# Hybrid decoder layer: the beginning and the cross attention in a written order, the memory's norm behind its projection, and the mLSTM's first gate chain and products at later places

## The chip, the cores and the metric

The kernel runs on one core of a Trainium2 chip. The metric is device time in microseconds (us) from one launch to its end, as a median over runs. The core has a matrix engine (TensorE, PE in the profile, whose weight loads are listed as PEld), a vector engine (VectorE, DVE), an engine for activations (ScalarE, ACT), a general one (GpSimd, POOL), and SyncE (SP), which here issues nearly all transfers. Every engine works through its own queue of instructions in order and waits on semaphores.

## The reference

One decoder layer on a sequence of 1024 tokens of width 1024 and a memory of 256 tokens, all in float32:

```python
h = rms_norm(x, norm_mix_g)
mq, mk, mv, mi, mf, mo, dq, dk, dv, cq = split(h @ w_in)
y_m = sigmoid(mo) * rms_norm(mlstm_chunkwise(silu(conv(mq, mk)), mv, mi, mf))   # 4 heads, chunks of 128
y_d = diff_attention(dq, dk, dv)                                                 # 8 heads, causal
mkv = rms_norm(mem, mem_norm_g) @ w_mem_kv
y_c = cross_attention(rms_norm(cq), rms_norm(mkv[:, :512]), mkv[:, 512:])        # 4 heads of 128, values 256 wide
g_m, g_d, g_c = split(sigmoid(h @ w_gate + b_gate))
x = x + (g_m * (y_m @ w_proj_m) + g_d * (y_d @ w_proj_d) + g_c * (y_c @ w_proj_c)) @ w_out
x = x + square(relu(rms_norm(x) @ w_up)) @ w_down
```

`rms_norm(v, g)` is v · rsqrt(mean(v²) + 1e-6) · g over the last axis. The change touches the norms of x and of the memory, the projection of the memory, cross attention, and the order in the mLSTM.

## The kernel before

**Split products.** A product of two float32 matrices is done in three passes (`mm3`, L121): each operand is split into a high part, rounded to fp32r, and a low part, the rest; PE adds high·high, high·low and low·high in PSUM. `split` (L111) and `split2` (L102) make the parts: ACT writes the high part (L115, or L118 with a scale), then DVE subtracts (L116, or L119). `load_w` (L142) loads a weight group in four raw pieces by SP (ring `rp`, 3 buffers) and splits each into a buffer of `wp` (4 buffers). Below, a "product" is one pass, one PE instruction of 512 columns in most places.

**Stages.** `consts` (L194) loads the vectors and transposes them, and computes lambda. `phase_x` (L299) is the beginning: it loads both tiles of memory (`mx`), normalises their rows in place (`norm_rows`, L240: a square on ACT with a sum, a power on POOL in `rsqrt_mean`, a multiply on DVE), and calls `mem_kv` (L248). That transposes the memory into `memT`, splits it with the norm's gain as scale, and projects it in three groups of 512 columns: one of K (`kr`, squared, normalised per head, transposed into `mkT`) and two of V (`mv`). x is loaded in eight tiles (`xk`), normalised row by row, and `half` transposes four tiles at a time into `hT`, the split and transposed h, in eight steps of 128 features. A score tile `sc` in PSUM holds two of these steps. Between the halves stands the second group of V's weights.

`branch_c` (L342) is cross attention. A stream of PE work (the query projection of eight tiles of 128 tokens, then 32 steps of merge-gate products) is cut into positions: a position is the three passes of one k. At positions given by a table, `weave` (L493) puts `turn` (normalised queries transposed), `scores` (L378: products, row maximum, four exponentials into `cpe`, and the softmax's division on DVE), `ptr` (the probabilities of one head transposed into `cpT`) and `values` (their product with `mv`, one score tile for each 128 columns, stored to HBM).

`branch_m` (L583) is the mLSTM, again a stream with a table. Its stream projects v, q and k and the output gates; the first 264-wide weight holds the input and forget gates too. `m_gates` (L505) begins with two transposes of `gi` and `gf` on PE and runs a long chain on DVE, ACT and two round trips through HBM, whose results are `g_b`, `g_w` and `g_a`, and rows that are stored to HBM (`g_dng`, `g_dwi`, `g_dd`) and loaded again. `m_gates2` (L575) transposes the three into `g_col`. Each of the eight half heads n then has items at a base position e plus an offset: `inter` (queries times the inter-chunk weight, `qp`), `decays` (the mask rows `ngb`), `krows` (weighted keys, `ks`), `scores`, four `chunk`s and three `final`s. `sc<-va,ks` and `sc<-va,mpT` are a chunk's state update and its numerator.

Behind these come the rest of the gates, the differential attention, the merge and the MLP, which the change leaves alone.

**What sets the order.** Instructions go through a scheduler that may reorder them within an engine unless they are kept in program order. In the kernel before, PE alone is pinned, and that in `branch_c` and `branch_m`; the order of ACT, DVE, SP and POOL, and PE's in the beginning, is the scheduler's. Buffers are handed out in rings (`rings`, L129), and a tile can be written once the readers of the one that had its buffer are done.

Of the kernel before, what the change touches and what calls it, by code (L numbers as in the profile page):

```python
# [71 lines left out]
class Layer:  # L72
    def __init__(self, tc, a, out):
        self.tc, self.nc, self.a, self.out = tc, tc.nc, a, out
        self.V, self.A = tc.nc.vector, tc.nc.scalar
        self.n = 0
# [117 lines left out]
    def consts(self, tmp):  # L194
# [32 lines left out]
        lv = tmp.tile([P, 256], F32, name="lamv")  # L227
        nc.sync.dma_start(lv, a["lamv"].partition_broadcast(P))
        pr = tmp.tile([P, 128], F32, name="lamp")
        l4 = lv.rearrange("p (a b) -> p a b", a=4)  # L230
        nc.vector.tensor_mul(pr[:, 0:64], l4[:, 0], l4[:, 1])
# [7 lines left out]

    def norm_rows(self, src, r1, scr):  # L240

        nc = self.nc
        nc.scalar.activation(scr, src, AF.Square, accum_out=r1)
        self.rsqrt_mean(r1, r1, D, 1)
        nc.vector.tensor_scalar_mul(src, src, r1)


    def mem_kv(self, pool, tmp, xs):  # L248
        nc, a = self.nc, self.a
        memT = tmp.tile([P, NK, 2, 256], F32R, tag="memT", name="memT")  # L250
        for k in range(0, NK, 2):
            ps = self.tp_tile()
            for i in range(2):
                for t in range(2):
                    nc.tensor.transpose(
                        ps[:, (i * 2 + t) * P : (i * 2 + t + 1) * P], xs[t][:, (k + i) * P : (k + i + 1) * P], self.ident
                    )
            for i in range(2):
                self.split(
                    memT[:, k + i, 0], memT[:, k + i, 1], ps[:, i * 256 : (i + 1) * 256],  # L260
                    self.vec[:, R_MEM + k + i : R_MEM + k + i + 1],
                )
        self.mkT = pool.tile([P, 4, 2, 256], F32R, name="mkT")
        self.mv = pool.tile([P, 2, 2, D], F32R, name="mv")

        def proj(w, t):
            ps = self.mm_tile()
            for k in range(NK):
                self.mm3(
                    ps, (memT[:, k, 0, t * P : (t + 1) * P], memT[:, k, 1, t * P : (t + 1) * P]), w[k], k == 0, k == NK - 1  # L270
                )
            return ps
# [26 lines left out]
    def phase_x(self, kv, tmp):  # L299
# [14 lines left out]
        for x in mem:  # L314
            norm(x)
# [1508 lines left out]
```

## Time and profile before

| | us |
|---|---|
| median of 3 runs | 2248.64 |
| lowest and highest | 2246.41, 2258.45 |
| the profiled execution | 2249.61 |
| its span, first to last instruction | 2247.8 |
| mean granted clock of TensorE | 0.993 |

All times in what follows are of the profiled execution unless a run is named. A row of the timeline gives start, length, engine, line, operation, output and inputs, shapes and count; what stands in brackets at its end is the engine's idle time ahead of it and who ended that. In a window's row, PEclk is the clock that TensorE was granted, in parts of full speed. The stages of the kernel before lie in the trace like this: the beginning to about 66 us, cross attention to 183, the mLSTM behind it.

### The profile page before, as it was taken

The numbers are of one execution on the slowest core, as the hardware profiler recorded it, in microseconds if no ns is written. First come the engines' busy times: TensorE is split into PE (matmuls) and PEld (weight loads), VectorE is DVE, ScalarE is ACT, GpSimd is POOL, SyncE is SP. The second block draws the span as 40 slices with busy tenths as digits, with TensorE's granted clock in tenths as the row PEclk, the third lists the DMA queues.
The fourth block names the chain that finished last, engine by engine and source line by source line (L and its number), as shares of the span: only waits on it lengthen the run. The fifth ranks groups of instructions, "written<-read, shape, count | busy, mean of one in ns | idle before, by whom it ended". The sixth has DMA issues, their size and how long they took to land.

```text
span 2247.8 us, 30530 instructions
## 1 busy us (share of the span) xinstructions
PE 2182.6 (97%) x11222; PEld 1877.5 (84%) x11222; DVE 1398.3 (62%) x2627; ACT 1019.8 (45%) x1994; POOL 540.4 (24%) x696
## 2 busy tenths in 40 slices
PE   7999899999999999999999999999899999899999
PEld 5778788988899999999888888887788888688777
DVE  6645366655138888888752232544588777865688
ACT  6533355444236666666542120323445444543232
POOL 2100000000011111111100002202666665665553
PEclk9999999999999999999999999999999999999999
DMA  6013122111311111110133443436445444844434
GB/s 246 20 71 113 44 87 78 54 60 52 119 55 34 34 31 38 38 36 29 61 128 135 134 148 117 141 103 206 153 143 186 151 155 162 296 163 147 154 118 169
DMA packets 113781, 247.89 MB, mean 110 GB/s; under 512 B 11066, under 2 KB 19551, under 8 KB 111583
## 3 DMA queue, kind: packets, MB, share of 16 engines
q1 hardware_dynamic: 111326, 233.36, 31.5%
q10 hardware_dynamic: 2304, 12.58, 1.4%
q8 instruction: 88, 1.44, 0.3%
q14 instruction: 63, 0.51, 0.1%
HBM read 178.76 MB, written 67.14 MB: 109 GB/s over the span
## 4 chain that ended last, share of the span: by engine, by line
PE 68%; DVE 14%; DMA 8%; ACT 5%; issue 2%; POOL 2%; SPq 0%; DVEq 0%; ACTq 0%; POOLq 0%
PE mm L91 40%; PE p L91 18%; PE sc L91 4%; PE tp L94 2%; PE po L91 2%; DVE sc L67 1%; DMA wraw<-in_wdown 1%; ACT dpe L67 1%; DVE wo L105 1%; DVE dpe L67 1%; PE pr L94 1%; DVE draw L67 1%; DVE dst L67 1%; DMA xr<-h_d 1%; DVE w L116 1%
## 5 line engine op out<-in xcount | busy, mean ns | idle before, releaser
L91 PE MATMUL mm<-hT,w 128*128 128x512 f32 x1920 | 466.4, 397 | 0.5 <-ACT gt L488 0.5
L91 PE MATMUL mm<-w,hT 128*128 128x384 f32 (+3 forms) x2496 | 459.3, 330 | 1.9 <-ACT w L115 1.6
L91 PEld LDWEIGHTS mm<-hT,w 128*128 128x128 f32 x1920 | 356.1, 189 | 76.0 <-ACT gt L488 1.7
L91 PEld LDWEIGHTS mm<-w,hT 128*128 128x128 f32 x2496 | 389.6, 189 | 12.1 <-ACT w L115 2.3
L91 PE MATMUL p<-xd,wo 128*128 128x512 f32 x1344 | 313.3, 394 | 16.5 <-DVE acc L1619 9.4
L91 PEld LDWEIGHTS p<-xd,wo 128*128 128x128 f32 x1344 | 253.5, 190 | 76.2 <-DVE acc L1619 12.8
L91 PE MATMUL p<-xo,wo 128*128 128x512 f32 x1344 | 309.5, 392 | 6.2 <-DVE st L1473 4.2
L91 PEld LDWEIGHTS p<-xo,wo 128*128 128x128 f32 x1344 | 253.2, 189 | 61.2 <-ACT pt L1286 4.6
L91 PE MATMUL mm<-kt,w 128*128 128x512 f32 x1152 | 261.8, 389 | 0.5 <-DVE w L116 0.5
L91 PEld LDWEIGHTS mm<-kt,w 128*128 128x128 f32 x1152 | 216.1, 188 | 46.1 <-DVE w L116 1.0
L104 ACT CAST wo<-wraw 128x896 fp32r<-128x896 f32 x122 | 114.9, 942 | 190.3 <-PE p L91 126.8
L105 DVE TENSOR_TENSOR wo<-wraw,wo 128x896 fp32r<-128x896 f32 x122 | 146.2, 1212 | 49.9 <-ACT wo L104 49.8
L1200 POOL TENSOR_TENSOR wraw<-wraw 128x128 f32<-128x128 f32 x128 | 99.0, 773 | 212.3 <-DMA wraw<-in_wdown 132.2
L115 ACT CAST w<-raw 128x256 fp32r<-128x256 f32 (+2 forms) x144 | 86.4, 619 | 140.1 <-PE mm L91 103.7
L67 ACT ACTIVATE dpe<-sc,dst,drr 128x256 f32<-128x256 f32 (+7 forms) x128 | 106.7, 833 | 62.2 <-DVE dst L67 51.6
L116 DVE TENSOR_TENSOR w<-raw,w 128x256 fp32r<-128x256 f32 (+2 forms) x144 | 100.5, 718 | 52.3 <-ACT w L115 52.3
L105 DVE TENSOR_TENSOR xd<-xd 128x1536 fp32r<-128x1536 f32 (+2 forms) x36 | 69.0, 1922 | 70.5 <-ACT xd L104 70.5
L67 DVE CUSTOM_DVE_ANT_0 sc<-sc,tmask 128x256 f32<-128x256 f32 (+7 forms) x128 | 97.0, 758 | 3.6 <-PE sc L91 2.4
L139 POOL TENSOR_SCALAR hss<-hss 128x4 f32<-128x4 f32 x8 | 3.3, 415 | 398.5 <-ACT mscr L767 398.5
L1201 POOL TENSOR_TENSOR wraw<-wraw 128x128 f32<-128x128 f32 x128 | 96.9, 757 | 0.0
L1202 POOL TENSOR_TENSOR wraw<-wraw 128x128 f32<-128x128 f32 x128 | 94.2, 736 | 0.0
L104 ACT CAST xd<-xd 128x1536 fp32r<-128x1536 f32 (+2 forms) x36 | 54.9, 1528 | 73.0 <-DMA xd<-r_d 73.0
(324 smaller groups left out, 3161.1 us busy)
## 6 DMA issues: line engine op xcount, KB each, us to landing
wraw<-in_wup SPq DMA_DIRECT2D x64, 256.0 KB, 3.2
r_d<-xts SPq DMA_DIRECT2D x16, 1024.0 KB, 4.3
wraw<-in_wdown SPq DMA_DIRECT2D x64, 256.0 KB, 3.1
xd<-r_d SPq DMA_DIRECT2D x19, 768.0 KB, 7.6
xd<-r_d SPq DMA_DIRECT2D x14, 1024.0 KB, 6.3
raw<-in_wgate SPq DMA_DIRECT2D x48, 256.0 KB, 3.0
gates<-gt SPq DMA_DIRECT2D x48, 256.0 KB, 2.1
raw<-in_wd SPq DMA_DIRECT2D x32, 384.0 KB, 3.1
```

The costliest lines, as they stand in the source:

```text
L67: return self.tc.keep_in_program_order(f(*a, **k))
L91: self.pin(self.nc.tensor.matmul(out, l, r, start=start, stop=stop))
L94: self.pin(self.nc.tensor.transpose(out, x, self.ident))
L104: self.A.copy(hi, src)
L105: low = lambda: self.V.tensor_sub(lo, src, f32(hi))
L115: nc.scalar.copy(hi, src)
L116: nc.vector.tensor_sub(lo, src, f32(hi))
L139: g.tensor_scalar(r, ss, 1.0 / width, EPS, op0=ALU.mult, op1=ALU.add)
L1200: G.tensor_add(r[:, 4], r[:, 0], r[:, 3])
L1201: G.tensor_sub(r[:, 5], r[:, 4], r[:, 1])
L1202: G.tensor_sub(r[:, 6], r[:, 1], r[:, 0])
```

## The change

It has four parts. The numbers of instructions stay as they were, but for a few on DVE.

**A written order.** A wrapper `InOrder` for SP, DVE and ACT keeps each instruction in program order. `phase_x` and `branch_c` use it, and `split2`, `split2s` and the new `w_raw` and `w_split` issue through it. The whole beginning is written out by hand:

```diff
+        w, rm = [], []
+        mem_turn(0)
+        w += self.w_split(raws[0][0], 512, 2)
+        mem_turn(2)
+        ps = [self.mm_tile() for _ in range(2)]
+        for k in range(NK):
+            for t in range(2):
+                proj(ps[t], w, k, t)
+            if k % 2 == 0 and k < 6:
+                w += self.w_split(raws[0][k // 2 + 1], 512, 2)
+                if k < 4:
+                    mem_turn(k + 4)
+            if k in (3, 5):
+                rm.append(square(mem[k // 4], "rm"))
...
+        rx = [square(x) for x in xs[0:4]]
+        for x, r in zip(xs, rx):
+            V.tensor_scalar_mul(x, x, r)
...
+        w = self.w_split(raws[1][0], 512, 2)
+        turn2(0, 0)
+        turn2(0, 2)
...
+            if k in (3, 5):
+                turn2(0, k + 1)
+                kr_turn(k // 4)
+            if k >= 4:
+                rx.append(square(xs[k]))
+            if k >= 6:
+                V.tensor_scalar_mul(xs[k - 2], xs[k - 2], rx[k - 2])
+        w2 = self.w_split(raws[2][0], 512, 2)
+        for i in (6, 7):
+            V.tensor_scalar_mul(xs[i], xs[i], rx[i])
```

`mem_turn(k)` transposes and splits two steps of memory, `turn2(hf, k)` two steps of x into one score tile, and `kr_turn` one tile of K. Cross attention's query weights are loaded and split here too, `wp` has 5 buffers, and lambda's arithmetic stands behind the beginning.

**The memory's norm behind its projection.** The raw memory is transposed, and the row's scale `rm` comes in where the products leave PSUM: as the scale of the copy and square of K, and of both parts of `mv` (`split2s`). K's four multiplies per tile become one with a broadcast.

**Cross attention.** `scores` ends with the exponentials; `probs`, the division, is an item of its own. Both value products of a head share one 1024-wide score tile. `cpe` has 8 buffers in place of 6, the first gate weights are loaded by eight items, and the first weights of the mLSTM may be loaded while cross attention runs (`self.wp.i = 11`).

```diff
+            add(8 * t + 21, probs, t)
+        for k in range(NK):
+            add(41 + 2 * k + k // 2, self.gate_load)
         for hf in range(2):
             for h in range(4):
-                b = (43, 78)[hf] + (4, 5)[hf] * h
+                b = (48 + 8 * h, 80 + 4 * h)[hf]
                 add(b, ptr, hf, h, 0)
-                add(b + 1, ptr, hf, h, 1)
-                add(b + 5, values, hf, h, 0)
-                add(b + 5, values, hf, h, 1)
+                add(b + 2 - hf, ptr, hf, h, 1)
+                add(b + 5 - 2 * hf, values, hf, h)
```

**The mLSTM's table.** Seven positions more for `m_gates2`, and other offsets for the first half head, with `decays` ahead of `inter`; three DVE instructions are pinned there, and the ones columns of `va` are written later.

```diff
-        add(96 + 8, self.m_gates2, gp)
+        add(96 + 15, self.m_gates2, gp)
...
-            kt, st, ch, fi = (9, 2, 14, 34) if n == 0 else (-2, 2, 7, 33) if n == 1 else (-16, -8, 3, 29)
+            kt, st, ch, fi = (18, 22, 26, 42) if n == 0 else (-2, 2, 7, 33) if n == 1 else (-16, -8, 3, 29)
...
-                add(e + 9, inter, hd, hf)
-                add(e + 9, decays, hd, hf)
-                st = 10
+                add(e + 16, decays, hd, hf)
+                add(e + 16, inter, hd, hf)
```

Where instructions stand now is shown at three places. First DVE's queue around the norm of x's second half, before: `xk` rows are the scaling of a tile of x, `hT` and `mv` rows low parts, `w_638` a weight's low part.

```order
L245 TENSOR_SCALAR xk_329<-xk_329,r_70_491 128x1024
L119 SCALAR_TENSOR_TENSOR hT<-sc_385,vec,hT 128x512
L119 SCALAR_TENSOR_TENSOR hT<-sc_398,vec,hT 128x512
L245 TENSOR_SCALAR xk_331<-xk_331,r_72_497 128x1024
L245 TENSOR_SCALAR xk_333<-xk_333,r_74_503 128x1024
L116 TENSOR_TENSOR mv<-mm_561,mv 128x512
L116 TENSOR_TENSOR w_638<-raw_636,w_638 128x1024
```

And the same place after, where `xk_270` and `xk_272` are the seventh and eighth tile and `w_482` is the first weight of V's second half.

```order
L67 TENSOR_TENSOR mkT<-tp_446,mkT 128x4x128
L67 TENSOR_SCALAR xk_266<-xk_266,r_66_422 128x1024
L67 TENSOR_SCALAR xk_268<-xk_268,r_70_453 128x1024
L67 TENSOR_TENSOR w_482<-raw_274,w_482 128x1024
L67 TENSOR_SCALAR xk_270<-xk_270,r_72_464 128x1024
L67 TENSOR_SCALAR xk_272<-xk_272,r_74_476 128x1024
L67 SCALAR_TENSOR_TENSOR mv<-mm_359,rm_221,mv 128x512
```

The weight's low part moved from behind all scalings to a place ahead of the last two.

Second ACT's queue at x's first half, before, with `hT` rows the high parts and the number behind `sc` the buffer of the score tile and its use.

```order
L243 ACTIVATE scr_69_486,r1_68_485<-xk_42_327 128x1024
L118 ACTIVATE hT_117<-sc_54_359,vec_76 128x512
L118 ACTIVATE hT_117<-sc_55_372,vec_76 128x512
L115 CAST w_61_467<-raw_60_465 128x1024
L115 CAST w_63_472<-raw_62_470 128x1024
L118 ACTIVATE hT_117<-sc_54_359,vec_76 128x512
L118 ACTIVATE hT_117<-sc_55_372,vec_76 128x512
```

After:

```order
L67 CAST w_56_330<-raw_26_258 128x1024
L67 ACTIVATE hT_108<-sc_57_333,vec_76 128x512 x2
L67 ACTIVATE hT_108<-sc_58_346,vec_76 128x512 x2
L67 CAST w_61_367<-raw_27_260 128x1024
L67 CAST w_62_383<-raw_28_262 128x1024
L67 ACTIVATE hT_108<-sc_63_393,vec_76 128x512 x2
```

Two score tiles took turns; now both high parts of a tile stand next to each other, and four of them ahead of the second weight.

Third PE's queue in the mLSTM from the last of the three gate transposes (`tp<-ident,g_a`) on, before: `mm<-hT,w` are three passes of the stream, `cv` the convolved keys, `qh,kh` the scores.

```order
L579 MATMUL tp_319_2340<-ident_64,g_a_2100 128x32
L91 MATMUL mm_320_2346<-hT_117,w_307_2284 128x512 x3
L94 MATMUL tp_324_2363<-ident_64,cv_298_2215 128x128 x4
L91 MATMUL mm_320_2346<-hT_117,w_308_2287 128x512 x3
L91 MATMUL tp_326_2380<-qh_295_2184,kh_300_2223 128x128 x12
L91 MATMUL mm_320_2346<-hT_117,w_310_2292 128x512 x3
L91 MATMUL mm_320_2346<-hT_117,w_311_2295 128x512 x3
L91 MATMUL mm_320_2346<-hT_117,w_313_2300 128x512 x3
L91 MATMUL mm_320_2346<-hT_117,w_314_2303 128x512 x3
L91 MATMUL sc_330_2411<-va0_1733,ks_325_2368 128x258 x3
L91 MATMUL sc_330_2411<-va0_1733,mpT_327_2394 128x258 x3
```

After, from the same transpose to the scores and shortly behind them:

```order
L656 MATMUL tp_312_2346<-ident_64,g_a_2084 128x32
L92 MATMUL mm_311_2324<-hT_108,w_308_2293 128x512 x3
L92 MATMUL mm_317_2371<-hT_108,w_299_2268 128x512 x3
L92 MATMUL mm_317_2371<-hT_108,w_300_2271 128x512 x3
L95 MATMUL tp_318_2378<-ident_64,cv_290_2199 128x128 x4
L92 MATMUL mm_317_2371<-hT_108,w_302_2276 128x512 x3
L92 MATMUL mm_317_2371<-hT_108,w_303_2279 128x512 x3
L92 MATMUL mm_317_2371<-hT_108,w_305_2284 128x512 x3
L92 MATMUL mm_317_2371<-hT_108,w_306_2287 128x512 x3
L92 MATMUL tp_320_2404<-qh_287_2168,kh_292_2207 128x128 x12
```

The transposes stood ahead of a tile's first step and now stand seven steps later, ahead of its last, and seven steps in place of two lie between them and the scores.

290 lines of the change are left out of this document (165 added, 125 removed).

## The prediction

> **What bounds the kernel now.** I read the page's first sections, then TensorE's waits, then its timeline where the change acts. First the page's span line, its busy times and its chain that ended last.
>
> ```profile
> span 2247.8 us, 30530 instructions
> PE 2182.6 (97%) x11222; PEld 1877.5 (84%) x11222; DVE 1398.3 (62%) x2627; ACT 1019.8 (45%) x1994; POOL 540.4 (24%) x696
> PE 68%; DVE 14%; DMA 8%; ACT 5%; issue 2%; POOL 2%; SPq 0%; DVEq 0%; ACTq 0%; POOLq 0%
> ```
>
> TensorE (PE) is busy in all but 2247.8 − 2182.6 = 65.2 us, so a change that leaves its products alone can win only in those 65 us and where products run slowly. The next view is PE's waits between 0 and 600 us (whom it waited for: total us, times, longest), and the heaviest wait behind 310 us.
>
> ```profile
> PE tp L204 <- DMA vraw<-in_vecs: 7.0, 1, 7.0
> PE tp L255 <- DVE mx L245: 5.0, 2, 4.8
> PE sc L91 <- ACT cpe L392: 3.9, 2, 2.0
> PE sc L91 <- ACT mpT L115: 3.1, 1, 3.1
> PE tp L579 <- ACT g_b L560: 2.9, 1, 2.9
> PE mm L91 <- ACT w L115: 1.6, 2, 1.1
> PE tp L94 <- DVE cpe L399: 1.6, 1, 1.6
> ...
> PE p L91 <- DVE acc L1619: 9.4, 8, 1.8
> ```
>
> The last row belongs to a stage that the change doesn't touch. The rows above it are what the change can reach: the memory's norm (5.0), cross attention's softmax (3.9 and 1.6), the first weights of the mLSTM (1.6), its gate chain (2.9) and the first chunk's numerator (3.1). Together that is 18 us. Behind three of these waits the clock falls. The windows below give us, PE, PEld, DVE, ACT, POOL busy, PEclk, DMA share and GB/s.
>
> ```profile
> 113.07:118.68 5.61, 5.61 (x20) 4.48 (x21) 2.69 (x7) 1.01 (x2) 0.00 (x0) 0.70 0.25 93
> 240.41:244.19 3.78, 3.78 (x14) 3.09 (x14) 0.26 (x1) 1.06 (x3) 0.00 (x0) 0.55 0.40 85
> 251.90:257.94 6.04, 6.04 (x16) 4.71 (x16) 2.36 (x6) 2.55 (x9) 0.00 (x0) 0.52 0.24 80
> ```
>
> Their losses are 5.61 × 0.30 = 1.7, 3.78 × 0.45 = 1.7 and 6.04 × 0.48 = 2.9 us, hidden in busy time.
>
> **The change part by part: the beginning.** The rows of PE's timeline are start, length, operation, shapes and count, with the wait ahead of it in brackets.
>
> ```profile
> 14.54 4.50 PE L91 MATMUL mm<-w,memT 128*128 128x512 f32 x10
> 66.08 5.29 PE L91 MATMUL mm<-w,hT 128*128 128x512 f32 x22
> 71.21 0.60 PE L94 MATMUL tp<-ident,cqr 128*128 128x128 f32 x4
> ```
>
> A 512-wide product costs (71.21 − 66.08) / 22 = 0.233 us warm and about 0.43 in the first ten. At 66.08 the cross attention had 14 products of its own behind it, so "before" reaches its first product, with everything ahead done, at 66.08 − 14 × 0.233 = 62.8 us. That is the figure to beat. PE's own work up to there is 144 products × 0.233, plus 88 transposes at some 0.09, or 41.5 us. ScalarE (ACT) and VectorE (DVE) prepare it by these pieces:
>
> ```profile
> 0.72 1.28 ACT L234 ACT_TABLE_LOAD   x1 [0.72 <-PEq L1813]
> 12.07 0.28 DVE L206 COPY vec<-tp 128x128 f32<-128x128 f32 x1
> 20.03 0.48 DVE L119 SCALAR_TENSOR_TENSOR memT<-tp,vec,memT 128x256 fp32r<-128x256 f32 x1 [1.57 <-ACT memT L118]
> 20.55 0.47 ACT L118 ACTIVATE memT<-tp,vec 128x256 fp32r<-128x256 f32 x1 [0.55 <-DVE memT L119]
> 30.82 0.59 ACT L278 COPY kr<-mm 128x512 f32<-128x512 f32 x1
> 40.68 1.06 ACT L243 ACTIVATE scr<-xk 128x1024 f32<-128x1024 f32 x1
> 42.77 0.75 DVE L245 TENSOR_SCALAR xk<-xk,r 128x1024 f32<-128x1024 f32 x1
> 42.48 1.27 ACT L118 ACTIVATE hT<-sc,vec 128x512 fp32r<-128x512 f32 x2 [0.65 <-PE sc L94]
> 43.44 1.40 DVE L119 SCALAR_TENSOR_TENSOR hT<-sc,vec,hT 128x512 fp32r<-128x512 f32 x2
> 43.63 1.99 ACT L115 CAST w<-raw 128x1024 fp32r<-128x1024 f32 x2
> 44.76 2.35 DVE L116 TENSOR_TENSOR w<-raw,w 128x1024 fp32r<-128x1024 f32 x2
> ```
>
> The memory's projection no longer waits for the norm, which gains little: the vectors land at 7.0, their transpose and copy end at 7.8, and ACT's table load, now behind that copy in ACT's order, ends at 9.1. Two high parts of one score tile alternate with the low parts (the 0.55 us wait at 20.55), so the second ends 1.5 later. A cast (1.0) and its low part (1.2) give the first full K product at 12.9, against 14.54. The 48 K products, ten of them cold, and the memory's last transposes end at about 27.1; the K copy at 30.82 was the same point before. This part gains 3.7.
>
> Then it turns. ACT now runs in the written order: 8 high parts with their waits (8 × 1.03), 4 casts (4.0) and 6 squares (6.4) behind 9.1 end at about 28. From a square's start to the scaled row takes 42.77 − 40.68 + 0.75 = 2.84, so the fourth row of x is ready at 30.2, and PE, done at 27.1, stands for 3.1. Behind the squares stand four operations on K (about 2.0), then the first cast of V's weights: the first V product comes at 32.7. The next two casts are written behind four high parts of hT. A pair writes from one score tile, so I take its second high part to wait for the first's low part: 0.64 + 0.70 + 0.64 + 0.70 = 2.7 a pair. "Before" alternated two tiles, so no row shows this wait at hT; its bounds are 0 and 0.70 a pair, and I take the upper, because the memT rows show it on one tile. That makes the second quarter's weights late by 3.0 (38.3 against 35.3). The rest of V's first half ends at 49.0. The squares of x's second half end at 51.6, and DVE is to scale the seventh and eighth row only behind the low part of the next weights (1.2): the last is ready at 55.3, and PE stands for 6.3. After that its transposes run cold (0.7 lost), two more quarters of weights are late by 2.2 and 2.3 behind hT pairs, and 24 products bring the cross attention's first product to about 73.1.
>
> So the beginning ends 73.1 − 62.8 = 10.3 us later than before, and I take 10.7 with some cold clock. Its bounds: if no wait behind the first product were left, 12.9 + 41.5 = 54.4, a gain of 8.4; if the clock falls behind each of the four stands, a loss of about 15.
>
> **Cross attention.** Its weights are split before it starts, the first gate weights come one by one, and the probability transposes, the softmax scaling and the value products stand later.
>
> ```profile
> 102.70 0.33 PE L94 MATMUL tp<-ident,cpe 128*128 128x128 f32 x1 [1.58 <-DVE cpe L399]
> 113.07 1.89 PE L91 MATMUL sc<-cpT,mv 128*128 128x512 f32 x6 [1.96 <-ACT cpe L392]
> 131.65 1.66 PE L91 MATMUL sc<-cpT,mv 128*128 128x512 f32 x6 [1.96 <-ACT cpe L392]
> ```
>
> ```profile
> raw<-in_wgate SPq DMA_DIRECT2D x48, 256.0 KB, 3.0
> ```
>
> The last row is a DMA issue: count, size, median us to landing. The first half's items stand 5 to 17 positions of 3 × 0.233 = 0.7 us later, and these waits go: 1.58 + 1.96 + 1.96, 0.2 of small ones and the 1.7 of clock, 7.4 in all. What is late next: three mLSTM weights are now cast on ACT ahead of the last tile's exponentials, each behind its own transfer. PE's value products of the last heads' first half need a score tile that those exponentials hold. With a transfer of 3.0 us, like a gate weight's, I put 1.4 on that wait (bounds 0 and 3). Net gain 6.0. The small edits I cost at nothing: lambda's arithmetic behind the beginning, the later ones columns, and one multiply of K in place of four lie on DVE (62% busy) under PE's products, and would cost under 1 us if that cover were gone, by the 0.75 us of the scaling row for the longest of them.
>
> **The mLSTM's start and gate chain.**
>
> ```profile
> 183.24 0.39 PE L91 MATMUL mm<-w,hT 128*128 128x264 f32 x1 [0.50 <-ACT w L115]
> 187.32 22.05 PE L91 MATMUL mm<-w,hT 128*128 128x264 f32 x174 [1.13 <-ACT w L115]
> 210.60 0.27 PE L94 MATMUL tp<-ident,gi 128*32 128x128 f32 x1
> 240.41 0.24 PE L579 MATMUL tp<-ident,g_b 32*128 32x32 f32 x1 [2.93 <-ACT g_b L560]
> 243.94 2.02 SPq L572 DMA_DIRECT2D g_dec<-g_dd  x1
> 251.90 1.31 PE L91 MATMUL sc<-va,mpT 128*128 128x258 f32 x3 [3.07 <-ACT mpT L115]
> ```
>
> The first weights are split during cross attention, so 0.50 + 1.13 and 0.2 more go: 1.9. The gate chain lasts from 210.60 to 240.4, 29.8 us. Its product on PE moves from 38 positions behind the chain's start to 45, and 45 × 0.7 = 31.5 covers it: 2.93 and 1.7 of clock go. Seven positions later it hides under the same projection products.
>
> The first numerator moves by 12 positions too, but what it waits for moves with it. ACT is written to evict a gate tile, whose buffer's store stands on SP behind the 2.02 us issue of the decays, before it exponentiates and splits the keys. I put its operand 15.0 us behind the chain's end and PE's arrival at 12, a wait of about 3 in place of 3.07. Bounds: none (the wait and its 2.9 of clock gone), or both as before. I take the clock's half. The gate chain and first chunk give 4.3 to 7.2, and I take 5.7.
>
> **The sum.** −6.0 − 1.9 − 5.7 + 10.7 = −2.9 us. Against the profiled execution's 2249.6 that is 2246.7; the median of the runs, 2248.6, lies 1.0 below it, so the forecast is 2246. What moves the clock is told by rows: waits of 2.93 and 3.07 halved it, and one wait of 1.96 did and the other did not. [...]
>
> **The rivals.** First, the beginning covers itself (faster). If the two high parts of a pair don't wait for the low one, and if the squares of x run in ACT's gaps, only the 3.1 us stand and some 0.5 of the 16.9 us of waits (3.1 + 3.0 + 6.3 + 2.2 + 2.3) remain. 13.3 less makes the loss of 10.7 a gain of 2.6, and the time 2246 − 13.3 = 2233. For it: ACT is busy only 45% of the span, and the alternating wait at hT stands in no row. Against it: ACT's own pieces add up to 28 us of the first 28.
>
> Second, the hoisted mLSTM weights come late (slower).
>
> ```profile
> raw<-in_wkv SPq DMA_DIRECT2D x12, 512.0 KB, 8.3
> ```
>
> Each of the three casts ahead of the last exponentials waits for a transfer that SP may issue only after an earlier split has freed a buffer, so they follow one another. At 3.0 us each PE hardly waits. At 8.3, as long as a weight takes in the beginning, the three cost 3 × 5.3 = 15.9 more, and the time is 2246 + 15.9 = 2262. It decides above 3.0 + 11.2 / 3 = 6.7 us a transfer, if cover is used up. For it: a written order gives ACT no way around a late transfer. Against it: in the window at 113 us the DMA engines are busy for 0.25 of the time.
>
> Third, the written order doesn't move what I say: if the chain of m_gates were not ahead of the numerator any more, its 5.7 would stay, 2252, still within the range.
>
> **How the numbers follow.** A measurement of this kernel tells 0.5% (11.2 us) from no change. The forecast's own terms (beginning 3 better to 4 worse, clock 3 each way, casts 3) give 2238 to 2257, within 0.5%, with a chance of 0.58 together with the third rival. The self-covering beginning has 0.28, since I rest 10 us on a written order whose small waits no row shows. The late weights have 0.14. The range reaches to the first rival's 2233 and most of the way to the second: 2232 to 2259, leaving out about 0.12 above and 0.06 below. Faster than 2237.4: 0.28. Slower than 2259.9: 0.14.
>
> **What would show it.** In the profile of the changed kernel: the first K product near 12.9; a stand of PE of about 6 us ahead of the second half's x transposes, with DVE's scaling of the eighth row behind a weight's low part; cross attention's first product near 73; no wait on a probability tile's scaling; no wait at the gate chain's transposes; and about 3 us at the first numerator. The prediction is wrong if cross attention starts before 65 (first rival), if ACT's exponentials stand over 5 us behind a weight cast (second), or if anything behind 310 us moves by more than 3 us.

## The result, and the profile after

The changed kernel takes 2269.07 us (median of 6 runs, 2264.5 to 2273.04) where the kernel before takes 2249.06 beside it (6 runs). The ratio is 1.0083 with a 95% interval of 1.0061 to 1.0105: slower by 20 us, outside the forecast range. Its profiled execution has 2266.09 us and a span of 2264.3, 16.5 over that of before; the other 3.5 us of the medians' difference lie in the spread of the runs, and the profiled one is among the faster.

Where the 16.5 us came from is read by cutting both spans at four instructions of TensorE that both programs have: the first query transposes of cross attention, the mLSTM's first product of 264 columns, its gate transposes, and the 66 products of the q and k projection behind the second half head. The columns are the stretch, its length, the busy time of PE, PEld, DVE, ACT and POOL, PEclk, DMA share and GB/s. First the kernel before:

```profile
0.00:71.21 71.21, 56.26 (x270) 44.23 (x270) 50.20 (x86) 48.57 (x78) 15.07 (x35) 1.00 0.60 207
71.21:183.24 112.03, 105.76 (x542) 87.37 (x540) 49.63 (x101) 48.91 (x120) 9.13 (x15) 0.98 0.14 53
183.24:210.60 27.36, 25.92 (x198) 24.78 (x199) 16.48 (x72) 12.69 (x37) 0.00 (x0) 1.00 0.45 147
210.60:314.87 104.27, 96.95 (x451) 79.26 (x450) 56.34 (x150) 43.34 (x116) 1.20 (x2) 0.95 0.22 67
314.87:2247.80 1932.93, 1897.67 (x9767) 1641.86 (x9765) 1225.68 (x2220) 866.26 (x1645) 515.03 (x645) 1.00 0.34 112
```

and the changed kernel:

```profile
0.00:85.79 85.79, 62.96 (x270) 49.24 (x271) 49.15 (x74) 47.96 (x74) 15.48 (x35) 0.94 0.49 168
85.79:202.62 116.83, 106.00 (x542) 86.63 (x540) 54.84 (x134) 52.06 (x134) 9.44 (x15) 0.99 0.19 64
202.62:227.47 24.85, 24.85 (x199) 24.49 (x198) 11.13 (x42) 9.34 (x27) 0.00 (x0) 1.00 0.39 114
227.47:329.31 101.84, 95.60 (x452) 77.34 (x451) 56.95 (x150) 43.13 (x116) 1.33 (x2) 0.98 0.22 69
329.31:2264.30 1934.99, 1899.81 (x9767) 1643.93 (x9765) 1226.47 (x2220) 867.45 (x1645) 516.38 (x645) 0.99 0.34 112
```

Row by row that is +14.6 in the beginning, +4.8 in cross attention, −2.5 at the mLSTM's start, −2.4 in the gate chain and the first two half heads, and +2.1 in the rest, whose instructions the change leaves alone. Of the 14.6, PE's idle time has 7.9 (85.79 − 62.96 against 71.21 − 56.26) and its busy time 6.7 (62.96 − 56.26, for the same 270 instructions, at a granted clock of 0.94 in place of 1.00). In cross attention PE has the same work and stands for 10.8 us where it stood for 6.3.

The waits of PE in the changed kernel, first up to the end of the beginning, then in cross attention:

```profile
PE sc L95 <- DVE xk L67: 8.6, 7, 2.6
PE tp L205 <- DMA vraw<-in_vecs: 7.2, 1, 7.2
PE mm L92 <- ACT w L67: 3.5, 3, 1.7
PE mm L92 <- DVE w L67: 3.0, 6, 0.8
PE tp L95 <- DMA mx<-in_mem: 0.5, 1, 0.5
```

```profile
PE tp L95 <- DVE cpT L67: 6.4, 3, 2.2
PE tp L95 <- ACT cqr L67: 4.0, 4, 1.1
```

The memory's norm (5.0 before) is gone, and the scaling of x's rows (0.6 before) costs 8.6. In cross attention the waits that the forecast wanted gone are gone, and 10.4 us of two new kinds stand there. ScalarE's queue shows why. In the changed kernel, at the second tile of queries:

```profile
91.50 0.57 ACT L67 ACTIVATE cpe<-sc,cmx,cr 128x256 f32<-128x256 f32 x1 [4.39 <-DVE cmx L67]
...
93.14 0.56 ACT L67 ACTIVATE cpe<-sc,cmx,cr 128x256 f32<-128x256 f32 x1
...
93.69 0.59 ACT L67 COPY cqr<-mm 128x512 f32<-128x512 f32 x1
```

and on TensorE:

```profile
89.70 3.57 PE L92 MATMUL mm<-w,hT 128*128 128x512 f32 x15
94.33 0.66 PE L95 MATMUL tp<-ident,cqr 128*128 128x128 f32 x4 [1.05 <-ACT cqr L67]
```

The copy `cqr` of a finished query tile stands behind the four exponentials of the tile before, so the transposes that read it come 1.05 us late, four times. In the kernel before ScalarE had them the other way round:

```profile
76.09 0.59 ACT L358 COPY cqr<-mm 128x512 f32<-128x512 f32 x1 [2.42 <-PE mm L91]
...
77.07 0.57 ACT L392 ACTIVATE cpe<-sc,cmx,cr 128x256 f32<-128x256 f32 x1
```

The 6.4 us (`cpT`) have a like cause. The instructions that wait are again query transposes. The PSUM tile that they write comes from a ring of two (`tp`), and both tiles hold transposed probabilities until VectorE has taken their low parts, which follow ScalarE's casts:

```profile
126.01 0.57 ACT L67 ACTIVATE cpe<-sc,cmx,cr 128x256 f32<-128x256 f32 x1 [3.87 <-DVE cmx L67]
...
129.44 1.10 ACT L67 CAST cpT<-tp 128x512 fp32r<-128x512 f32 x2
```

```profile
130.98 0.77 PE L95 MATMUL tp<-ident,cqr 128*128 128x128 f32 x4 [2.24 <-DVE cpT L67]
```

TensorE transposed these probabilities at 124.92 and 126.75; ScalarE casts them at 129.44, behind four exponentials, a copy, a square and a weight's cast.

### The profile page after: what moved, and what is told of

Read it like the earlier page. It is cut to its first block, busy times and chain, and to the rows that moved or that the text cites. A ratio compares the mean times of both kernels' runs of the same rounds, so it can differ in the third digit from the quotient of the medians.

```text
span 2264.3 us, 30502 instructions
## 1 busy us (share of the span) xinstructions
PE 2189.2 (97%) x11222; PEld 1881.6 (83%) x11222; DVE 1398.5 (62%) x2619; ACT 1019.9 (45%) x1994; POOL 542.6 (24%) x696
## 4 chain that ended last, share of the span: by engine, by line
PE 63%; DVE 14%; DMA 7%; ACT 4%; issue 2%; POOL 2%; SPq 0%; DVEq 0%; ACTq 0%; POOLq 0%
PE mm L92 37%; PE p L92 18%; PE sc L92 3%; PE tp L95 2%; PE po L92 2%; DMA wraw<-in_wdown 1%; DVE sc L67 1%; ACT dpe L67 1%; DVE wo L106 1%; DVE dpe L67 1%; DVE draw L67 1%; PE pr L95 1%; DVE dst L67 1%; DMA xd<-r_d 1%; DMA xr<-h_d 1%
## 5 line engine op out<-in xcount | busy, mean ns | idle before, releaser
L116 ACT CAST w<-raw 128x256 fp32r<-128x256 f32 (+2 forms) x128 | 69.9, 569 | 134.5 <-PE mm L92 120.3
L117 DVE TENSOR_TENSOR w<-raw,w 128x256 fp32r<-128x256 f32 (+2 forms) x128 | 81.1, 654 | 48.7 <-ACT w L116 48.4
```

Of the source, the lines that this page charges most:

```text
L116: nc.scalar.copy(hi, src)
L117: nc.vector.tensor_sub(lo, src, f32(hi))
```

## The experiments

My theory after the result: both losses are ones of order on ScalarE and VectorE. In the beginning the squares and scalings of x stand late, and in cross attention the exponentials stand ahead of work that TensorE needs sooner. The rivals: the loss comes from TensorE's own written order, from the norm behind the projection, or from the positions of the table. The table gives each run by the same cuts, in us of its one profiled execution, and the ratio of its runs to those of the kernel before beside it, with the 95% interval. How far a single execution can be trusted is seen where kernels share a stage: four with the same written beginning reach the query transposes between 85.79 and 86.66 (changed, c_late_exp, c_ptr_first, c_sched), and the rest, the same in all, takes 1928.52 to 1937.48.

| kernel | first query transposes | cross attention | to the gate transposes | to the 66 products | the rest | ratio |
|---|---|---|---|---|---|---|
| before | 71.21 | 112.03 | 27.36 | 104.27 | 1932.93 | |
| changed | 85.79 | 116.83 | 24.85 | 101.84 | 1934.99 | 1.0083 (1.0061 to 1.0105) |
| old_begin | 70.00 | 115.19 | 26.82 | 103.46 | 1930.03 | 1.0014 (1.0002 to 1.0026) |
| c_late_exp | 86.19 | 107.53 | 24.86 | 101.31 | 1930.01 | 1.0031 (1.0017 to 1.0046) |
| c_ptr_first | 85.84 | 103.55 | 24.86 | 101.46 | 1932.09 | 1.0003 (0.9992 to 1.0015) |
| c_sched | 86.66 | 108.24 | 24.85 | 101.81 | 1930.44 | 1.0018 (1.0002 to 1.0034) |
| m_only | 70.75 | 111.97 | 27.27 | 103.23 | 1929.78 | 0.9994 (0.9985 to 1.0004) |
| x_sched | 71.28 | 118.50 | 24.73 | 101.66 | 1935.23 | 1.0012 (0.9998 to 1.0026) |
| x_v_first | 88.15 | 116.85 | 24.86 | 101.16 | 1937.48 | 1.0076 (1.0054 to 1.0099) |
| x_mul_first | 84.10 | 116.96 | 24.85 | 102.67 | 1928.52 | 1.0071 (1.0047 to 1.0096) |
| x_two_tiles | 84.81 | 116.99 | 24.85 | 102.00 | 1929.25 | 1.0054 (1.0038 to 1.0070) |
| best_old | 71.34 | 103.54 | 27.71 | 102.19 | 1933.72 | 0.9954 (0.9937 to 0.9970) |
| best_sched | 70.90 | 103.45 | 25.53 | 103.06 | 1936.66 | 0.9951 (0.9932 to 0.9969) |
| best_ch | 71.38 | 103.55 | 25.31 | 101.41 | 1934.25 | 0.9945 (0.9927 to 0.9963) |

### The beginning of the kernel before in the changed kernel

In the table this is old_begin.

```diff
-        mem = [load(a["mem"][t * P : (t + 1) * P, :], "mx") for t in range(2)]
-        raws = [self.w_raw(a["wkv"][0], 512, 2)]
...
+        for x in mem:
+            norm(x)
+        gen = self.mem_kv(kv, tmp, mem)
```

> The changed kernel with the beginning of the kernel before (its loads, its norm ahead of the projection, the scheduler's order; cross attention's weights loaded at its start); cross attention and the mLSTM as changed. If the written beginning alone costs what the two traces show (first query product at 77.6 us against 62.8), the first query product comes at 62 to 64 us and the span is 2264.3 - 14.8 = 2249.5 us, about that of the kernel before. If part of the 14.8 us was owed to what follows (TensorE's clock or transfers shared with cross attention), less than 10 us comes back. Cross attention itself should take 125 us as in the changed kernel, not 120.

The query transposes come at 70.00, 15.8 us sooner (the first query product, 36 products ahead, at about 61.6), and the span is 2245.5, 18.8 less. Of the 18.8, 5.0 lie in the untouched rest. The whole loss of the beginning comes back, and little behind it depends on it: cross attention takes 1.6 us less and keeps its 4.1 and 6.4 us of waits, the mLSTM's start is 2.0 longer (26.82), and the gate stretch 1.6.

### Only ScalarE's and VectorE's order in the beginning given back

In the table this is x_sched.

```diff
-        self.S, V, A = (InOrder(self.tc, e) for e in (nc.sync, nc.vector, nc.scalar))
+        self.S, V, A = InOrder(self.tc, nc.sync), nc.vector, nc.scalar
```

> The changed kernel, but in the beginning ScalarE's and VectorE's order is again the scheduler's; TensorE and SyncE stay in the written order. Theory: the beginning's 14.6 us come from the order of those two queues (squares and scalings of x directly ahead of the transposes that need them); then the first query transposes, at 85.8 us in the changed kernel and 71.2 before, come at 75 to 80. Rival: TensorE's written order itself (all 16 transposes of x in one block, with no product of V between them, ahead of V's products) is the cause, then they stay within 2 us of 85.8.

TensorE's instructions stand in the very same order as in the changed kernel, and the memory's norm is still behind its projection; yet the query transposes come at 71.28, better than expected. So the 14.6 us are the order of the two queues, and neither TensorE's order nor the moved norm. (Cross attention takes 118.50 here, 1.7 more than in the changed kernel, with the same waits and a granted clock of 0.97 in place of 0.99, so 12.8 us of the gain reach the mLSTM.) What the scheduler does differently is seen on ScalarE, here in this kernel:

```profile
17.28 1.06 ACT L263 ACTIVATE scr<-xk 128x1024 f32<-128x1024 f32 x1
...
18.67 0.47 ACT L245 ACTIVATE memT<-tp,vec 128x256 fp32r<-128x256 f32 x1 [0.24 <-DVE memT L246]
19.05 1.05 ACT L263 ACTIVATE scr<-xk 128x1024 f32<-128x1024 f32 x1
```

and at the same place in the changed kernel:

```profile
16.50 0.47 ACT L67 ACTIVATE memT<-tp,vec 128x256 fp32r<-128x256 f32 x1 [1.61 <-PE tp L95]
17.52 0.47 ACT L67 ACTIVATE memT<-tp,vec 128x256 fp32r<-128x256 f32 x1 [0.55 <-DVE memT L67]
...
20.82 0.48 ACT L67 ACTIVATE memT<-tp,vec 128x256 fp32r<-128x256 f32 x1 [1.88 <-PE tp L95]
```

The squares of x fill the gaps of 1.6 and 1.9 us in which ScalarE waits for TensorE; in the written order these gaps stay open, and the first square of x starts at 25.25 in place of 17.28. (No run moves the squares alone: that they are the larger part of the loss is argued from these rows.) TensorE then has x's transposes ready at 27.59 with no wait, where the changed kernel shows this:

```profile
31.08 0.33 PE L95 MATMUL sc<-ident,xk 128*128 128x128 f32 x1 [1.14 <-DVE xk L67]
32.55 3.04 PE L95 MATMUL sc<-ident,xk 128*128 128x128 f32 x13 [1.14 <-DVE xk L67]
...
57.57 0.48 PE L95 MATMUL sc<-ident,xk 128*128 128x128 f32 x1 [2.60 <-DVE xk L67]
58.39 3.03 PE L95 MATMUL sc<-ident,xk 128*128 128x128 f32 x13 [0.35 <-DVE xk L67]
```

### V's first products ahead of x's norm

In the table this is x_v_first.

```diff
-        rx = [square(x) for x in xs[0:4]]
-        for x, r in zip(xs, rx):
-            V.tensor_scalar_mul(x, x, r)
+        w = self.w_split(raws[1][0], 512, 2)
         kr, r4 = [], []
...
+        w += self.w_split(raws[1][1], 512, 2)
+        rx = [square(x) for x in xs[0:4]]
...
```

> The changed kernel with V's first two quarters of weights split, and K's evictions, ahead of the squares of x's first half on ScalarE, and on TensorE V's first 24 products ahead of the first transposes of x. If TensorE's idle block at 28 to 35 us comes from x's norm standing between K's last product and V's first, then 4 to 5 us go: the first query transposes at 81 to 82 us and the span at about 2260. Rival: VectorE and ScalarE are full in the beginning and the wait only moves to x's transposes or to V's second weights; then less than 2 us go.

88.15, 2.4 us later than the changed kernel: the rival holds. TensorE fills the idle block with 24 products of V, but then waits 9.4 us for `xk` in all (8.6 before this edit), and the second half of x, which this edit leaves alone, is as late as ever. Another written order does not by itself repair the first.

### The seventh and eighth scaling ahead of a weight's low part

In the table this is x_mul_first.

```diff
-        w2 = self.w_split(raws[2][0], 512, 2)
         for i in (6, 7):
             V.tensor_scalar_mul(xs[i], xs[i], rx[i])
+        w2 = self.w_split(raws[2][0], 512, 2)
```

> The changed kernel with the scaling of x's seventh and eighth tile ahead of the low part of V's second weights on VectorE, in place of behind it. The prediction named that low part (1.2 us) as what makes them late. Theory: the last scaling ends 1.2 us earlier and the first query transposes come at 84.6 us in place of 85.8. Rival: the scaling waits for the power on GpSimd, or the weights' low part is late in turn; then within 0.4 us of 85.8.

84.10, 1.7 us sooner, but only half of that is the edit's. This execution was 1.1 us ahead before the edited place (the first of the second half's transposes of x stands at 52.15, and at 53.25 in the changed kernel). From that transpose to V's first product behind the block it takes 7.01 us here and 7.83 in the changed kernel, as in the three others with the same order there (7.83 to 7.84). So the step of the prediction stands, with 0.8 us in place of 1.2.

### Two score tiles in turn

In the table this is x_two_tiles.

```diff
+        def turn4(hf, k):
+            f = [x_turn(hf, k + i) for i in range(4)]
+            for i in (0, 2, 1, 3):
+                f[i]()
...
-        turn2(0, 0)
-        turn2(0, 2)
+        turn4(0, 0)
```

> The changed kernel with the first four steps of x written so that ScalarE takes a step of each of two score tiles in turn. The prediction priced the wait of a tile's second high part for its first low part at 0.7 us a pair; the trace shows 0.8 to 0.9. Theory: the two waits of 0.9 us at 35 to 37 us go and V's second weights come 1.5 us earlier: query transposes at 84.3 us in place of 85.8. Rival: those weights' place is taken by another wait (the scaling of x, the power on GpSimd): within 0.4 us of 85.8.

84.81, 1.0 us sooner, between theory and rival; 0.5 of that stood before the edited place (x's first transposes at 27.78 in place of 28.24). From V's first product to the fifth step of x it takes 7.47 us, and 7.99 to 8.05 in the changed kernel and the three others with the same order: 0.5 us. The waits for the second weights there (0.87 and 0.77) are gone, but the 24 products ran at a clock of 0.78. The wait of a second high part for the first low part is real, and small: 0.8 and 0.5 us together are a tenth of the beginning's loss. The rest goes with the scheduler's order, where the squares stand earlier.

### The exponentials behind the next tile's query copy

In the table this is c_late_exp.

```diff
...
+            add(8 * t + 16, exps, t)
             add(8 * t + 21, probs, t)
```

> The changed kernel with the four exponentials of a score tile as an item of their own at position 8t+16, behind the copy of the next tile's queries on ScalarE. Theory (ScalarE's written order): the four waits of TensorE's query transposes for the query copy (4.0 us) go, those for the low parts of the transposed probabilities (6.4 us) stay; cross attention takes 121 us in place of 125.0 and the span is about 2260 us. Rival (the waits come from the transposes' own buffers or from the late start): cross attention stays at 125. Second rival (the score tile is held 1.2 us longer and the value products wait for it, as in the kernel before): 3.9 us of waits for the exponentials come back, cross attention 124 to 125.

Cross attention takes 107.53, 9.3 us less, 5 more than expected. The four waits for `cqr` are gone, and those for `cpT` are halved, to 3.3, which I had not expected. Copy and square of a query tile (1.2 us) now run while VectorE takes the row maximum, and so the casts of the transposed probabilities behind them come that much sooner too:

```profile
120.75 0.58 ACT L67 COPY cqr<-mm 128x512 f32<-128x512 f32 x1 [2.73 <-PE mm L92]
...
121.72 0.57 ACT L67 ACTIVATE cpe<-sc,cmx,cr 128x256 f32<-128x256 f32 x1
...
124.18 1.10 ACT L67 CAST cpT<-tp 128x512 fp32r<-128x512 f32 x2
```

From the row maximum's start to that cast it is 4.1 us (120.05 to 124.18) and was 5.0 (124.41 to 129.44). The other 2.3 us are in the products themselves: PE's busy time falls from 106.00 to 103.71. The second rival, the score tile held longer, did not come.

### The probability transposes ahead of the exponentials as well

In the table this is c_ptr_first.

```diff
-                add(b, ptr, hf, h, 0)
-                add(b + 2 - hf, ptr, hf, h, 1)
+                c = (46 + 8 * h, 80 + 4 * h)[hf]
+                add(c, ptr, hf, h, 0)
+                add(c + 1, ptr, hf, h, 1)
```

> As the kernel with the late exponentials, and the first half's probability transposes at 46+8h and 47+8h in place of 48+8h and 50+8h, so that ScalarE casts them ahead of the exponentials. Theory: both groups of waits go (4.0 and 6.4), cross attention takes 125.0 - 10.4 = 114.6 us, under the 119.9 of the kernel before, and the span is about 2254 us. Rival (buffers): as the kernel with the late exponentials. If the transposes now wait for the softmax's division (the kernel before had 1.6 us of that), 116.

103.55, a further 4.0 less, and the 6.4 us of waits are gone but for 0.9 at the softmax's division; expected was 114.6 by a cut 8.2 us ahead of this one, which is 106.4 here. PE is busy for nearly all of it:

```profile
85.84:189.39 103.55, 102.66 (x541) 86.32 (x540) 55.44 (x134) 52.50 (x134) 9.22 (x15) 1.00 0.22 72
```

With this edit the changed kernel is level with the kernel before, though its beginning is still 14.6 us late.

### The scheduler's order in cross attention, positions as changed

In the table this is c_sched.

```diff
-        V, A = self.V, self.A = InOrder(self.tc, nc.vector), InOrder(self.tc, nc.scalar)
-        self.S = InOrder(self.tc, nc.sync)
+        V, A = nc.vector, nc.scalar
```

> The changed kernel with ScalarE, VectorE and SyncE in the scheduler's order in cross attention, all positions as changed. The scheduler puts the query copy ahead of the exponentials. Theory: the four waits for the query copy (4.0 us) go as with the late exponentials; the casts of the transposed probabilities still stand behind exponentials, so 3 to 6 us of waits for their low parts stay: cross attention 107 to 113 us from the first query transposes, against 116.8. Rival: the positions alone make both waits: 116 to 117.

108.24, as expected: no wait for `cqr`, and 3.5 for `cpT`. Everything else that the change does in cross attention (positions, buffers, weights split ahead), with the scheduler's order, is 3.8 us better than the kernel before (112.03), and the written order takes 8.6 from that. But the mended written order, 103.55, is better than the scheduler's here; the early transposes with the scheduler's order were not run.

### The mLSTM's table alone in the kernel before

In the table this is m_only.

```diff
-        add(96 + 8, self.m_gates2, gp)
+        add(96 + 15, self.m_gates2, gp)
...
-            kt, st, ch, fi = (9, 2, 14, 34) if n == 0 else (-2, 2, 7, 33) if n == 1 else (-16, -8, 3, 29)
+            kt, st, ch, fi = (18, 22, 26, 42) if n == 0 else (-2, 2, 7, 33) if n == 1 else (-16, -8, 3, 29)
...
```

> The kernel before with the mLSTM's new offsets and its three pinned instructions alone. By the trace of the changed kernel (104.3 us from the gate transposes to the second half head's end against 101.8) the gate chain's wait and its slow clock go (2.9 + 1.7) but about 2 comes back at the numerator and the first output: span 2247.8 - 2.4 = 2245.4 us. By the prediction's own terms it is 5.7 less, 2242. If the numerator's wait takes over all of it, 2247 to 2248.

103.23 against 104.27: 1.0 us, where 2.4 was expected. The span is 4.8 us less, but 3.2 of that lie in the untouched rest, and the runs tell no difference from the kernel before (0.9985 to 1.0004). The gate chain's wait is gone, the numerator still waits 3.3, and the first output has a new wait of 1.0.

### The parts that won, together

The first kernel is best_old in the table.

> The beginning of the kernel before, cross attention as changed with the late exponentials and the early probability transposes, the mLSTM as changed. If the parts add up: query transposes at 70 to 71 us, cross attention 103.6 us from there (111.5 in the kernel before), mLSTM to the second half head's end about 128.3 (131.6 before), the rest 1930 to 1935: span 2233 to 2237, a time of about 2237 us, 12 under the kernel before. Rival: the mLSTM's first weights, loaded during a shorter cross attention, come late (1.7 us of that is seen with the old beginning already), 2239 to 2241.

2239.94 us against 2248.13 beside it, with a span of 2238.5. The parts add up, except for 2.9 us at the mLSTM's start (27.71 in place of 24.85). The rival had the size, and in part the cause:

```profile
182.37 0.40 ACT L116 CAST w<-raw 128x256 fp32r<-128x256 f32 x1 [0.88 <-DMA raw<-in_wmo]
```

```profile
182.80 0.42 DVE L117 TENSOR_TENSOR w<-raw,w 128x256 fp32r<-128x256 f32 x1 [0.82 <-ACT w L116]
```

```profile
183.52 6.72 PE L92 MATMUL mm<-w,hT 128*128 128x264 f32 x53 [2.62 <-DVE gf L663]
```

The weights that TensorE multiplies with there are in time. Late are those of the output gates (`in_wmo`), which the stream needs only later: the two engines stand at their splits, and `gf`, the last reader of the first tile of products, comes only behind them, at 183.22. The third tile of products waits for that. In old_begin the same wait is 1.7 us.

The second is best_sched.

> The changed kernel with ScalarE and VectorE in the scheduler's order in the beginning, and cross attention with the late exponentials and the early probability transposes. If the parts found so far add up: query transposes at 71.3 us, 103.6 us from there to the mLSTM's first weights, 24.8 to the gate transposes, 101.6 to the second half head's end, 1930 to 1935 behind: span 2231 to 2236, a time 12 to 16 us under the kernel before. Rival: the mLSTM's first weights come late when cross attention ends earlier, as with the old beginning (27.7 in place of 24.8): 3 us more.

2240.22 against 2251.01, with cross attention and beginning as expected. The mLSTM's parts are 0.7 and 1.5 us longer than expected and the untouched rest 1936.66, so the span, 2239.6, is over the expected range; 0.4 of the 0.7 is again a wait for `gf`, and why the other part is longer isn't shown.

The third, best_ch, differs from best_sched in this:

```diff
-            kt, st, ch, fi = (18, 22, 26, 42) if n == 0 else (-2, 2, 7, 33) if n == 1 else (-16, -8, 3, 29)
+            kt, st, ch, fi = (18, 22, 31, 47) if n == 0 else (-2, 2, 7, 33) if n == 1 else (-16, -8, 3, 29)
```

> As best_sched, with the first half head's chunks and outputs five positions later (31 and 47 in place of 26 and 42). The prediction put the numerator's operand 3 us behind TensorE's arrival, and the changed kernel shows 3.3 us of wait and a slow clock behind it. If the operand's chain runs free of TensorE, five positions of 0.7 us cover the 3.3: the wait goes, with 1 to 2 us of clock, and the stretch from the gate transposes to the second half head's end takes 97 to 98 us in place of 101.5. Rival: the chain waits for something that moves along, as it did between the kernel before and the changed one (3.07 and 3.27 in spite of twelve positions): within 1 us of 101.5.

2238.58 against 2251.01, the best of all kernels here, though from best_sched its runs can't be told (2238.07 to 2241.4 there, 2235.41 to 2243.29 here). The stretch to the 66 products is 101.41, where theory had 97 to 98 and the rival 100.5 to 102.5. Still, the operand's chain runs free of TensorE, as the theory had it: the numerator's wait fell from 3.27 to 0.47 and 0.23. What keeps the time up is that the second chunk now waits:

```profile
246.20 0.50 PE L92 MATMUL sc<-va,mpT 128*128 128x258 f32 x2 [0.47 <-ACT mpT L116]
...
253.93 1.26 PE L92 MATMUL sc<-Ch,qp 128*128 128x258 f32 x3 [3.13 <-ACT Ch L116]
```

ScalarE shows what stands ahead of the state's cast:

```profile
252.31 1.28 ACT L799 ACTIVATE ngb<-ngb,g_col 128x128 f32<-128x128 f32 x4 [5.57 <-DVE ngb L790]
253.49 0.39 ACT L116 CAST Ch<-C 128x258 fp32r<-128x258 f32 x1
```

and VectorE what they wait for:

```profile
251.52 0.69 DVE L790 TENSOR_TENSOR ngb<-ngb,tmaskT 128x512 f32<-128x512 f32 x1 [4.65 <-DMA ngb<-g_dng]
```

The mask rows `ngb` are the next half head's, whose place I had not moved. SyncE issued their load at 247.13, directly behind the store of a gate tile at 246.76, and VectorE stood 4.65 us for it. The exponentials on ScalarE wait for that, the cast of the state behind them waits along, and so does the copy of the state that stands behind the mask rows on VectorE (252.13). It is the same fault as in cross attention, made by my own edit; 1.7 us are left of the 4 expected.

## Why the prediction was wrong

**The beginning: the waits were right, the slow clock behind them was mis-sized.** Forecast was a loss of 10.7, measured 14.6. TensorE's stands were where they were put: the first K products at 11.84 and 13.10 (12.9 forecast), V's first product behind x's norm at 35.24 (32.7), the eighth row behind the weight's low part at 58.3 (55.3), the first cross attention product at 77.62 (73.1). From 11.84 to 77.62 they add up to 13.4 us, less than the 16.9 that the forecast had. What was too small is TensorE's own time between them: it is busy for 52.4 us with 144 products and 80 transposes, and the forecast had 43.3 (73.1 − 12.9 − 16.9). I priced the slow clock behind the stands at 1.1 (0.7 for cold transposes and 0.4 in the sum); the granted clock is 0.92 over this stretch and 0.50 in two blocks of transposes. A part of the 9.1 is also that transposes which stood alone lasted longer (0.33 us for the one at 31.08, where the four at 44.11 took 0.36 up to the next product, 0.09 each). The range's "about 15" had this in. One stand was also put too early: I let each scaled row follow its square and did not see that the rows pace each other at 1.47 us:

```profile
28.80 0.75 DVE L67 TENSOR_SCALAR xk<-xk,r 128x1024 f32<-128x1024 f32 x1 [0.72 <-POOL r L141]
30.27 0.75 DVE L67 TENSOR_SCALAR xk<-xk,r 128x1024 f32<-128x1024 f32 x1 [0.72 <-POOL r L141]
31.74 0.75 DVE L67 TENSOR_SCALAR xk<-xk,r 128x1024 f32<-128x1024 f32 x1 [0.72 <-POOL r L141]
```

The fourth row came at 32.5 in place of 30.2 (a last square of 1.06 that ends at 28, and 2.84 from its start, would have given 29.8): a part is this pace, and a part that ScalarE's squares ended at 29.5 and not at 28. The first rival, a beginning that covers itself, fell, since a written order gives ScalarE no way to use its gaps; with the scheduler's order for ScalarE and VectorE it came true (71.28).

**Cross attention: the sign was wrong.** The failed step is "What is late next: three mLSTM weights", with its 1.4 us and "Net gain 6.0". The removed waits did go, but what came next was not the weights. It was the query copy behind the exponentials (4.0) and the probabilities' casts behind exponentials, copy, square and weights (6.4), two terms that the forecast doesn't have. I read each moved item at its position on TensorE and didn't read, for each engine, what the new program order puts ahead of what; the copy's place was not in the table, but in the stream. The two edits that mend just this order give 13.3 us back, and the net gain would have been 8.5 by these cuts (112.03 − 103.55), more than I claimed for the change.

**The mLSTM's start** gained 2.5 (1.9 forecast), and its mechanism holds: in the changed kernel TensorE is busy for all of its 24.85. The second rival (weights that land late at the exponentials) fell.

**The gate chain** gained 2.4 of the 5.7. The wait at the transposes is gone, as computed:

```profile
266.24 0.69 ACT L565 ACTIVATE gt<-mm,dv 128x512 f32<-128x512 f32 x1 [9.04 <-DMA gates<-gt]
...
272.65 0.62 ACT L116 CAST mpT<-ngb 128x512 fp32r<-128x512 f32 x1 [1.07 <-DVE ngb L804]
```

and the rows above show the predicted cause of the numerator's wait: a gate tile's tanh stands 9.0 us behind a store, which SyncE issues at 260.65, directly behind the decays' transfer at 260.27, and the operand `mpT` starts 6.4 later. The wait is 3.27, about 3 forecast. What was missed are the waits behind it: 1.0 at the first output and 0.7 at the second half head (0.2 before). And the slow clock behind the numerator stayed, of whose 2.9 the forecast took half: the 12 products behind it take 4.50 us at a granted clock of 0.61, in the kernel before 5.10 at 0.53, and a chunk later 2.93 at 1.00. The 5.7 is also not the sum of its terms, which is 6.1 (2.93, 1.7 and half of 2.9). The third rival, that the 5.7 would stay, is half right in its size: 3.3 of it stayed.

**The rest** was to move by less than 3 us, and moved by 2.1; other kernels with the same instructions there spread from 1928.5 to 1937.5, so this is no effect of the change.

Of the sum, the sign of cross attention is 10.8 us of error (−6.0 to +4.8), the beginning 3.9, the chain 3.3, the mLSTM's start −0.6, and the rest 2.1: together 19.5, from −2.9 to 16.5. The 3 us each way that the forecast's range has for the clock are shown by no run; measured were, in the beginning alone, 6.7 us more of TensorE's busy time for the same 270 instructions, at a granted clock of 0.94 in place of 1.00.

## What to carry to other kernels

When a table of positions also becomes the program order of the side engines, write out each engine's queue around every wait of the busy engine and ask what stands directly ahead of the instruction it waits for; a long item that nobody needs soon (here four exponentials of 2.2 us, or squares) belongs behind a short one that someone does. A written order forgoes the filling of gaps that a scheduler does: fix the order of the engine that bounds the kernel, and fix the others only where the traces show a conflict. Here the scheduler's order was better in the beginning (71.28 against 85.79), and the written one, once mended, in cross attention (103.55 against 108.24). And an engine at 45% of the span can still be the bound of a stage.

## What the runs showed of the hardware

In the norm of x GpSimd's small operation took 0.19 us at 26.47, where VectorE was idle, and 0.75 us at 30.32, beside a multiply of VectorE that took 0.75 as well:

```profile
26.47 0.19 POOL L140 TENSOR_SCALAR r<-r 128x1 f32<-128x1 f32 x1 [0.20 <-ACT scr L67]
...
30.32 0.75 POOL L140 TENSOR_SCALAR r<-r 128x1 f32<-128x1 f32 x1
31.16 0.55 POOL L141 TENSOR_TENSOR r<-r,mhalf 128x1 f32<-128x1 f32 x1
```

The multiply lasts from 30.27 to 31.02 and the small operation to 31.07; the power needs its result, and the next multiply waits for the power: 1.47 us a row. What lengthened the small operation these rows don't show.

TensorE's granted clock was 0.50 behind short stands that came close together. Behind three waits of at most 1.14 us between 28 and 33 us, and again behind four (1.22, 1.09, 2.60 and 0.35) between 52 and 58, the 13 transposes ran at that clock (it is the third number from the end):

```profile
32.55:35.24 2.69, 2.69 (x14) 2.69 (x14) 2.69 (x4) 0.87 (x2) 1.81 (x4) 0.50 0.00 0
58.39:61.08 2.69, 2.69 (x14) 2.69 (x14) 1.87 (x3) 0.69 (x1) 0.00 (x0) 0.50 0.46 163
```

Behind a single wait of 1.05 us, ahead of the query transposes at 94.33, it was 1.00 (94.33 to 98.33); in the kernel before it was 1.00 too behind the second of the two waits of 1.96 (131.65 to 136.00). The block of 16 transposes, up to the next product, took 7.0 us (28.24 to 35.24) with 3.4 of waits in it, and 1.7 in x_sched (27.59 to 29.26), where it ran without a wait. So here the stands came with a loss of 5.3 us, 1.9 more than their own length.
